# A second copy of each head's high key part: by ScalarE before, by a DMA inside SBUF now

## The chip, the cores and the metric

The kernel runs on one core of one Trainium2 chip, in one launch. The metric is the device time of an execution in microseconds (us). TensorE (PE in the profile, PEld its weight loads), VectorE (DVE), ScalarE (ACT), GpSimd (POOL) and SyncE (SP) run side by side, each through its own list of instructions in order; SP is the engine whose queue starts all of this kernel's DMA transfers.

## The reference, cut to what matters

The kernel computes two decoder layers on 512 tokens of width 1024 in float32: a token mixer, a squared-ReLU MLP and a gated embedding in each layer.

```python
# layer 0: heads A (stick-breaking) and B (differential); layer 1: heads C (three dilated windows)
z  = jnp.einsum('bqhd,bkhd->bhqk', qa_b, ka) * scale          # A
sc = jnp.einsum('bqhmd,bkhmd->bhmqk', qb_b, kb) * scale       # B, plus a bias by distance
sc = jnp.einsum('bqchd,bkchd->bhcqk', q_s, k_s) * scale       # C, plus a bias by distance
...
h = h + mixer(rmsnorm(h)); h = h + square(relu(rmsnorm(h) @ w_up)) @ w_down
h = h + (p @ w_proj) * sigmoid(rmsnorm(h) @ w_gate)
```

Every head has 64 numbers per token for its queries and its keys. The change touches how the keys are laid out for the products q k.

## The kernel before, in words

Every float32 operand is split into a high part, rounded to the format that TensorE multiplies fast (fp32r), and a low part, the rest. Products use three matmuls (high x high, low x high, high x low; `mm3`, L135). ScalarE makes the high part of a weight block (L122) and GpSimd the low part in two halves (L126).

For the scores of a head the parts are stacked instead. A query tile `qq` has 128 partitions: the head's 64 high numbers in one half, its 64 low numbers in the other. The key tile `kh` must then hold the high key part in both halves, so that one matmul gives high x high plus low x high (L498); a second matmul against `klz`, which holds the low key part in one half and zeros in the other, gives the rest (L499). `evacuate` (L462) makes these tiles. Its line L465 takes a product out of PSUM into `f` (`tmp` in the profile): 128 partitions, two heads of 64. For each of the two heads L479 writes the high part into the half where the head lies (`kh[a]`), L480 writes the same numbers into the other half (`kh[b]`), both on ScalarE, and L481 makes the low part on VectorE. Five `kh` buffers take turns.

Each layer's mixer has four groups: layer 0 differential, differential, stick-breaking, stick-breaking; layer 1 four dilated groups. A group projects values, queries and keys (`project`, L401) from three weight blocks of 1 MB and then attends (`attend`, L547): 16 steps of scores, softmax, transposes and products with the values. While one group attends, the projection of the next one runs between its steps (`interleave`, L157). A group has two key products, so four heads, and there are eight groups: L480 runs 32 times. In the first group of a layer the keys come before the values, in all others the keys come last and the group's first scores follow at once.

The framework sets a fixed order for each engine when the kernel is built. TensorE's order mixes the next projection into the scores, and an instruction that must wait holds up all that stands behind it on its engine. On SP the same holds for transfers: a weight load into one of two `raw` buffers (L114) waits until ScalarE and GpSimd have split the block that lay there. Each pair of scores banks in PSUM is freed by VectorE (L515, softmax heads) or ScalarE (L582 and L583, stick-breaking heads). In a differential head `subnorm` (L607) squares on ScalarE (L610, L611) for a matmul over partitions (L614, L615).

Of the kernel before, what the change touches and what calls it, by code (L numbers as in the profile page):

```python
# [12 lines left out]
F32 = mybir.dt.float32  # L13
F32R = mybir.dt.float32r
I32 = mybir.dt.int32
AF = mybir.ActivationFunctionType
# [46 lines left out]
def trunk(  # L63
# [5 lines left out]
    nc = tc.nc  # L69
    uid = [0]  # L70

    def nm(s):
        uid[0] += 1
        return f"{s}_{uid[0]}"
# [15 lines left out]
    def t2k(tag, pool=None, dtype=F32):  # L90
        return (pool or (mix[0] if tag in ("tmp", "tmp2") else spool)).tile([P, S], dtype, tag=tag, name=nm(tag), bufs=T_BUFS.get(tag, 2))
# [274 lines left out]
    def mixer(layer, norm, nxt):  # L366
# [34 lines left out]
        def project(g, cur):  # L401
# [38 lines left out]
            def queries_keys():  # L440
                qscale = -0.5 * HD ** -0.5 if kind == "sb" else 0.5 * HD ** -0.5
                qk, waiting = [], []
                for isq in (True, False):
                    src = next_block()
                    lo_eng[0] = nc.vector if start else nc.gpsimd
                    blk = blk0 if isq and start and not layer else block(src, KT, P)
                    lo_eng[0] = nc.gpsimd
                    accs = [ps_wide() if start else ps("mm") for _ in range(2)]
                    if start and isq:
                        yield from lin_units(accs, blk, ahl, 0, KT, True)  # L450
                        waiting = accs
                        continue
                    for i, acc in enumerate(accs):
                        yield from lin_units([acc], [blk[i]], ahl, 0, KT, False)
                        if waiting:
                            statistics()
                            for x, held in enumerate(waiting):
                                evacuate(True, x, held, qk, qscale)
                            waiting = []
                        evacuate(isq, i, acc, qk, qscale)  # L460

            def evacuate(isq, i, acc, qk, qscale):  # L462
                rstd = stat["rstd"]
                f = t2k("tmp")
                nc.vector.scalar_tensor_tensor(f, acc, qscale if isq else -0.5, rstd, op0=ALU.mult, op1=ALU.mult)  # L465
                lower, upper = slice(0, 64), slice(64, 128)
                if isq:
                    qq = []
                    for a, b in ((lower, upper), (upper, lower)):
                        q = mpool.tile([P, S], F32R, tag="qq", name=nm("qq"), bufs=6)  # L470
                        nc.scalar.activation(q[a], f[a], AF.Copy)
                        nc.vector.tensor_tensor(q[b], f[a], q[a].bitcast(F32), op=ALU.subtract)
                        qq.append(q)
                    qk.append(qq)
                else:
                    for s, (a, b) in enumerate(((lower, upper), (upper, lower))):
                        kl = klz[s][kl_i[0] % KLB]
                        kh = mpool.tile([P, S], F32R, tag="kh", name=nm("kh"), bufs=5)
                        nc.scalar.activation(kh[a], f[a], AF.Copy)  # L479
                        nc.scalar.activation(kh[b], f[a], AF.Copy)  # L480
                        nc.vector.tensor_tensor(kl[a], f[a], kh[a].bitcast(F32), op=ALU.subtract)  # L481
                        heads.append((qk[i][s], kh, kl))
                    kl_i[0] += 1
# [535 lines left out]
```

## Time and profile before

| | us |
|---|---|
| three timed runs | 1310.06, 1311.92, 1312.02 |
| their median | 1311.92 |
| the profiled execution, whole | 1310.61 |
| its span from first to last instruction | 1308.8 |
| TensorE busy in the span | 1285.2 (98%) |
| VectorE busy | 977.6 (75%) |
| ScalarE busy | 687.5 (53%) |
| GpSimd busy | 193.0 (15%) |

The span is cut into 40 slices on the profile's page; TensorE shows 9 tenths or more in all but the last one, so what a change is worth lies in TensorE's short waits. The two mixers lie in about 15 to 255 us and 670 to 890 us of the span. An engine that is busy half of the time can still decide a wait where its instructions bunch: ScalarE shows 6 and 7 tenths in the slices of the first mixer. Bracketed text behind a row of the timeline is the engine's idle time before that instruction and who ended it.

### The profile page before, as it was taken

The page shows a single profiled execution, that of the slowest core. Times are in us where ns is not written, and L with a number is a line of the kernel's source. Part 1 is how long each engine was busy: PE and PEld are TensorE (multiplying, and loading weights), DVE is VectorE, ACT ScalarE, POOL GpSimd, SP SyncE. Part 2 cuts the span into 40 slices and gives each one's busy share as a digit, 9 for nine tenths or more (in the row PEclk, how much of TensorE's full clock was granted, in tenths as well). Part 3 has the DMA queues.
Part 4 walks back from the last instruction along what each step waited for, and adds up shares of the span by engine and source line. Part 5 has one row for each costly group of instructions (what it writes and reads, how often), then busy time and mean ns, then how long its engine had stood idle before and what let it go on. Part 6 is the DMA issues. An engine that isn't in the chain of part 4 may idle for free.

```text
span 1308.8 us, 18582 instructions
## 1 busy us (share of the span) xinstructions
PE 1285.2 (98%) x7256; PEld 1120.1 (86%) x7256; DVE 977.6 (75%) x1623; ACT 687.5 (53%) x1117; POOL 193.0 (15%) x160
## 2 busy tenths in 40 slices
PE   9999999999999999999999999999999999999997
PEld 7888797888998989988889899878899898898886
DVE  6688788768848859845667887887785785994566
ACT  6676768555535334244456667765453443433344
POOL 2333443410000000000023333322000000000001
PEclk9999999999999999999999999999999999999999
DMA  5421323223232322322433222212323223132241
GB/s 204 137 83 57 121 89 113 81 97 118 76 129 68 123 100 97 110 96 87 161 119 105 89 90 74 73 65 70 124 96 104 91 97 127 67 129 97 97 145 65
DMA packets 28040, 133.20 MB, mean 102 GB/s; under 512 B 3312, under 2 KB 4048, under 8 KB 15280
## 3 DMA queue, kind: packets, MB, share of 16 engines
q1 hardware_dynamic: 27952, 132.01, 29.1%
q8 instruction: 57, 0.93, 0.3%
q14 instruction: 31, 0.25, 0.1%
HBM read 125.63 MB, written 6.37 MB: 101 GB/s over the span
## 4 chain that ended last, share of the span: by engine, by line
PE 86%; DVE 7%; ACT 5%; issue 1%; DMA 1%; SPq 0%; DVEq 0%; ACTq 0%
PE mm L136 14%; PE mm L137 14%; PE mm L138 14%; PE tp L138 5%; PE tp L137 5%; PE tp L136 5%; PE sc L138 5%; PE sc L137 5%; PE sc L136 5%; PE pv L543 2%; PE tp L524 2%; PE pv L138 2%; PE pv L137 2%; PE pv L136 2%; PE sc L498 1%; PE sc L499 1%
## 5 line engine op out<-in xcount | busy, mean ns | idle before, releaser
L122 ACT ACTIVATE wh<-raw 128x1024 fp32r<-128x1024 f32 (+1 forms) x168 | 173.6, 1037 | 238.2 <-PE mm L137 74.6
L126 POOL TENSOR_TENSOR wl<-raw,wh 128x512 fp32r<-128x512 f32 (+1 forms) x132 | 180.2, 1388 | 309.2 <-ACT wh L122 290.0
L136 PE MATMUL mm<-hi,wh 128*128 128x512 f32 x564 | 222.8, 395 | 0.0
L137 PE MATMUL mm<-lo,wh 128*128 128x512 f32 x564 | 221.0, 392 | 0.6 <-DVE lo L177 0.6
L138 PE MATMUL mm<-hi,wl 128*128 128x512 f32 x564 | 220.9, 392 | 0.3 <-DVE wl L128 0.3
L128 DVE TENSOR_TENSOR wl<-raw,wh 128x1024 fp32r<-128x1024 f32 x102 | 124.4, 1222 | 40.6 <-ACT wh L122 34.1
L138 PEld LDWEIGHTS mm<-hi,wl 128*128 128x128 f32 x564 | 106.0, 188 | 23.8 <-DVE wl L128 0.7
L137 PEld LDWEIGHTS mm<-lo,wh 128*128 128x128 f32 x564 | 106.2, 188 | 20.9 <-DVE lo L177 1.3
L136 PEld LDWEIGHTS mm<-hi,wh 128*128 128x128 f32 x564 | 106.3, 188 | 20.2 <-ACT hi L176 0.7
L743 ACT ACTIVATE wh<-raw 128x1024 fp32r<-128x1024 f32 x48 | 50.7, 1057 | 69.8 <-PE sc L137 35.4
L138 PE MATMUL mm<-uh,wl 128*128 128x256 f32 (+1 forms) x288 | 87.3, 303 | 0.0
L137 PE MATMUL mm<-ul,wh 128*128 128x256 f32 (+1 forms) x288 | 87.1, 302 | 0.0
L136 PE MATMUL mm<-uh,wh 128*128 128x256 f32 (+1 forms) x288 | 86.4, 300 | 0.0
L518 ACT ACTIVATE e<-e,mn 128x128 f32<-128x128 f32 (+3 forms) x96 | 53.7, 560 | 43.5 <-DVE mn L515 43.2
L722 DVE TENSOR_TENSOR ul<-u,uh 128x1792 fp32r<-128x1792 f32 (+1 forms) x32 | 58.3, 1823 | 23.4 <-ACT uh L721 23.4
L721 ACT ACTIVATE uh<-u 128x1792 fp32r<-128x1792 f32 (+1 forms) x32 | 49.4, 1543 | 48.7 <-DVE u L717 48.4
L710 ACT ACTIVATE u<-u 128x512 f32<-128x512 f32 x64 | 39.4, 624 | 54.3 <-DVE u L709 51.3
L744 DVE TENSOR_TENSOR wl<-raw,wh 128x1024 fp32r<-128x1024 f32 x48 | 58.5, 1220 | 9.8 <-ACT wh L743 9.7
L138 PE MATMUL sc<-hi,wl 128*128 128x512 f32 x168 | 65.4, 389 | 0.0
L137 PE MATMUL sc<-lo,wh 128*128 128x512 f32 x168 | 65.4, 389 | 0.0
L136 PE MATMUL sc<-hi,wh 128*128 128x512 f32 x168 | 65.4, 389 | 0.0
L137 PE MATMUL mm<-wl,hi 128*128 128x256 f32 (+1 forms) x216 | 64.5, 299 | 0.7 <-DVE wl L128 0.7
(261 smaller groups left out, 3467.8 us busy)
## 6 DMA issues: line engine op xcount, KB each, us to landing
raw<-in_w_up_dram SPq DMA_DIRECT2D x32, 1024.0 KB, 4.9
raw<-in_w_down_dram SPq DMA_DIRECT2D x32, 1024.0 KB, 4.9
raw<-in_w_in_dram SPq DMA_DIRECT2D x23, 1024.0 KB, 4.9
raw<-in_w_gate_dram SPq DMA_DIRECT2D x8, 1024.0 KB, 4.9
bias<-urow SPq DMA_DIRECT2D x24, 256.0 KB, 3.5
raw<-in_w_outa_dram SPq DMA_DIRECT2D x8, 768.0 KB, 4.2
pj<-pjd SPq DMA_DIRECT2D x16, 256.0 KB, 4.7
h<-in_xT_dram SPq DMA_DIRECT2D x8, 256.0 KB, 5.6
```

The source lines that it names most:

```text
L122: nc.scalar.activation(hi, src, AF.Copy)
L126: nc.gpsimd.tensor_tensor(lo[:, kx], src[:, kx], hi[:, kx].bitcast(F32), op=ALU.subtract)
L128: nc.vector.tensor_tensor(lo, src, hi.bitcast(F32), op=ALU.subtract)
L136: nc.tensor.matmul(acc, lh, rh, start=start, stop=False)
L137: nc.tensor.matmul(acc, lh, rl, start=False, stop=False)
L138: nc.tensor.matmul(acc, ll, rh, start=False, stop=stop)
L518: nc.scalar.activation(e[:, 0:n], e[:, 0:n], AF.Exp, scale=-1.0, bias=mn, accum_out=s)
L710: nc.scalar.activation(ui, ui, AF.Square, scale=0.5)
L721: nc.scalar.activation(uh[:, parts], u[:, parts], AF.Copy)
L722: nc.vector.tensor_tensor(ul[:, parts], u[:, parts], uh[:, parts].bitcast(F32), op=ALU.subtract)
L743: nc.scalar.activation(hi, src, AF.Copy)
L744: nc.vector.tensor_tensor(lo, src, hi.bitcast(F32), op=ALU.subtract)
```

## The change

L480 becomes a DMA issued by SP. It copies the finished high part from its own half of the tile (`kh[a]`) to the other (`kh[b]`), 64 partitions of 2 KB, 128 KB in all. ScalarE loses 32 instructions, SP's queue gains 32 transfers, and each transfer waits for L479 of its head.

```diff
                         kh = mpool.tile([P, S], F32R, tag="kh", name=nm("kh"), bufs=5)
                         nc.scalar.activation(kh[a], f[a], AF.Copy)
-                        nc.scalar.activation(kh[b], f[a], AF.Copy)
+                        nc.sync.dma_start(kh[b].bitcast(F32), kh[a].bitcast(F32))
                         nc.vector.tensor_tensor(kl[a], f[a], kh[a].bitcast(F32), op=ALU.subtract)
```

The fixed order of the engines shifts with it. On ScalarE, in the first group of layer 0, the keys of the first product (`kh_348`, `kh_352`) and of the second (`kh_382`, `kh_386`) stand around the split of a weight block (`wh_665`):

```order
 L471 ACTIVATE qq_343<-tmp_338 64x512
 L479 ACTIVATE kh_348<-tmp_346 64x512
-L480 ACTIVATE kh_348<-tmp_346 64x512
 L479 ACTIVATE kh_352<-tmp_346 64x512
-L480 ACTIVATE kh_352<-tmp_346 64x512
 L122 ACTIVATE wh_665<-raw_547 128x1024
 L479 ACTIVATE kh_382<-tmp_380 64x512
-L480 ACTIVATE kh_382<-tmp_380 64x512
 L479 ACTIVATE kh_386<-tmp_380 64x512
-L480 ACTIVATE kh_386<-tmp_380 64x512
```

The split and the second product's keys have two copies fewer ahead of them, and what follows has four fewer.

On ScalarE again, where the third group of layer 0 starts, the output of a differential head (`o_206`) and its square (`tmp_328_1604`) stand behind the keys of that group:

```order
 L122 ACTIVATE wh_1641<-raw_1639 128x1024
 L479 ACTIVATE kh_1560<-tmp_1558 64x512
-L480 ACTIVATE kh_1560<-tmp_1558 64x512
 L479 ACTIVATE kh_1564<-tmp_1558 64x512
-L480 ACTIVATE kh_1564<-tmp_1558 64x512
 L597 ACTIVATE o_206<-pv_1571 128x512
 L610 ACTIVATE tmp_328_1604<-o_206 128x512
```

The output and its square have two copies fewer ahead of them.

On SP, where the second group of layer 1 starts (`raw` are weight blocks, `bias` the bias tiles of the scores, `kh_7166` the key tile of the group's first head):

```order
 L507 DMA bias_7498<-urow 128x512
 L114 DMA raw_7672<-in_w_in_dram 128x2048
+L480 DMA kh_7166<-kh_7166 64x512
+L480 DMA kh_7170<-kh_7170 64x512
+L480 DMA kh_7224<-kh_7224 64x512
+L480 DMA kh_7228<-kh_7228 64x512
 L507 DMA bias_7612<-urow 128x512
 L114 DMA raw_7828<-in_w_in_dram 128x2048
```

The four copies stand directly behind a weight load of 1 MB and ahead of the next bias tile. At the start of the third group of layer 1 they stand in the same way behind `raw_8267`, at the start of the fourth behind a load of 768 KB, `raw_8793`.

## Rows read from the trace of the kernel before

**Rows 1.** The page: TensorE's busy time, share of the span, instructions.

```profile
PE 1285.2 (98%) x7256; PEld 1120.1 (86%) x7256; DVE 977.6 (75%) x1623; ACT 687.5 (53%) x1117; POOL 193.0 (15%) x160
```

**Rows 2.** Waits of TensorE: engine, line waited for; us in total, times, longest.

```profile
PE sc L498 <- DVE v L436: 4.0, 2, 2.8
PE sc L498 <- DVE mn L515: 3.9, 4, 1.2
...
PE sc L498 <- ACT e L583: 1.3, 2, 0.9
PE pv L614 <- ACT tmp L611: 1.2, 1, 1.2
...
PE pv L615 <- DVE tmp L612: 0.5, 2, 0.2
```

**Rows 3.** The tile kh: line, engine, count, ns min/median/max, first and last start.

```profile
L480 ACT ACTIVATE kh<-tmp x32: 616/631/634, 39.5 to 851.4; 64x512 fp32r<-64x512 f32 x32
```

**Rows 4.** Windows: stretch, us, busy PE, PEld, DVE, ACT, POOL, PEclk, DMA.

```profile
44.60:48.06 3.46, 0.67 (x6) 0.47 (x5) 2.88 (x5) 2.31 (x5) 0.92 (x1) 1.00 0.39 104
48.06:51.47 3.41, 3.41 (x18) 3.41 (x18) 2.42 (x7) 0.70 (x2) 2.52 (x2) 0.50 0.66 264
704.97:708.40 3.43, 3.43 (x28) 3.43 (x29) 2.33 (x11) 2.00 (x6) 2.56 (x2) 1.00 0.60 248
```

**Rows 5.** Timeline, first group, ScalarE, GpSimd, VectorE, TensorE: start, us, instruction, [idle before].

```profile
41.42 1.06 ACT L122 ACTIVATE wh<-raw 128x1024 fp32r<-128x1024 f32 x1
...
42.56 2.96 POOL L126 TENSOR_TENSOR wl<-raw,wh 128x512 fp32r<-128x512 f32 x2 [5.54 <-ACT wh L122]
...
43.07 2.99 DVE L481 TENSOR_TENSOR klz<-tmp,kh 64x512 fp32r<-64x512 f32 x2 [0.69 <-ACT kh L479]
...
47.66 0.39 PE L498 MATMUL sc<-kh,qq 128*128 128x256 f32 x1 [2.79 <-DVE v L436]
```

**Rows 6.** Timeline, the same group a little later, VectorE and TensorE.

```profile
54.62 0.29 DVE L515 CUSTOM_DVE_ANT_0 e<-sc,bias 128x128 f32<-128x128 f32 x1 [2.46 <-DMA bias<-urow]
...
56.34 0.28 PE L498 MATMUL sc<-kh,qq 128*128 128x256 f32 x1
```

**Rows 7.** Timeline, TensorE's waits at later places of both mixers.

```profile
145.34 0.49 PE L614 MATMUL pv<-tmp,ones_r 128*128 128x512 f32 x1 [1.18 <-ACT tmp L611]
...
704.97 0.36 PE L498 MATMUL sc<-kh,qq 128*128 128x256 f32 x1 [1.20 <-DVE v L436]
...
852.83 0.44 PE L498 MATMUL sc<-kh,qq 128*128 128x384 f32 x1 [1.12 <-DVE mn L515]
```

**Rows 8.** Timeline of SP, the issues of one weight load and one small load.

```profile
45.54 0.35 SPq L114 DMA_DIRECT2D raw<-in_w_in_dram  x1
46.13 0.35 SPq L323 DMA_DIRECT2D tmp<-in_lambdas_dram  x1
```

**Rows 9.** Transfers issued in 45 to 52 us: count, KB each, us to landing.

```profile
raw<-in_w_in_dram SPq DMA_DIRECT2D x1, 1024.0 KB, 5.0
...
tmp<-in_lambdas_dram SPq DMA_DIRECT2D x1, 128.0 KB, 4.7
...
urow<-e SPq DMA_DIRECT2D x2, 8.0 KB, 1.5
```

**Rows 10.** Timeline, starts of layer 1's second and fourth group, SP and TensorE.

```profile
748.34 0.33 SPq L114 DMA_DIRECT2D raw<-in_w_in_dram  x1
...
751.86 0.28 PE L498 MATMUL sc<-kh,qq 128*128 128x256 f32 x1
...
844.12 0.33 SPq L114 DMA_DIRECT2D raw<-in_w_outa_dram  x1
...
848.98 0.28 PE L498 MATMUL sc<-kh,qq 128*128 128x256 f32 x1
```

**Rows 11.** Timeline, start of layer 0's second group, ScalarE and TensorE.

```profile
91.06 0.63 ACT L479 ACTIVATE kh<-tmp 64x512 fp32r<-64x512 f32 x1
...
96.56 0.28 PE L498 MATMUL sc<-kh,qq 128*128 128x256 f32 x1
```

## Prediction

> **What bounds the kernel now.** I read the page's busy times first. TensorE is busy for 98% of the span [rows 1], so an engine that is relieved shortens the kernel only where TensorE waits for it. The second view is therefore the list of TensorE's waits [rows 2]: all of them together are a dozen microseconds, and the groups that could be touched here are the scores (L498) waiting for VectorE's values L436 (4.0 us) and softmax L515 (3.9), the scores waiting for ScalarE's L583 (1.3), and the subnorm matmuls (1.2 and 0.5). The third view, the tile kh, gives the size of what goes [rows 3]. The fourth is the timeline around each of those waits [rows 5 to 7], read backwards: which instruction ended the wait, and do ScalarE's key copies stand ahead of it? Last I read SP's issues and landings [rows 8 to 11], because the copy becomes a transfer there.
>
> **What is removed.** 32 copies of 0.631 us [rows 3] are 20.2 us of ScalarE. Nearly all of it lies beside matmuls and is worth nothing. It counts at these places:
>
> First group of layer 0. TensorE waits 2.79 us for the values L436 [rows 5], which stand on VectorE behind the two low key parts L481. These two take 2.99 us together, and they end about half a microsecond after GpSimd's weight split (42.56 + 2.96 = 45.52 against 43.07 + 2.99 = 46.06), more than twice what ScalarE needs for two of that size; I read this as GpSimd holding VectorE up. GpSimd starts when ScalarE's L122 (41.42, no idle time before it) is done, and two of the removed copies stand right ahead of L122. So the split, the low key parts and the values all move up by 2 x 0.63 = 1.3 us. Gain 1.3, bounds 0 (something else ends VectorE's delay) and 2.6 (all four removed copies count).
>
> Behind that wait TensorE's granted clock is 0.50 for 3.41 us [rows 4], the lower of its two levels (1.2 instead of 2.4 GHz): 1.7 us lost. Ahead of it TensorE had been busy for only 0.67 of 3.46 us. With a wait of 1.5 us I expect the clock to stay up, since behind the wait of 1.20 us that ends at 704.97 [rows 7] it was 1.00 [rows 4]; between 1.2 and 2.8 us nothing shows where it turns. The gain is not all kept. The third pair of scores (56.34) needs a PSUM bank that L515 frees at 54.62 + 0.29 = 54.9, and L515 waited for its bias tile [rows 6]. TensorE would now arrive 3.0 us earlier, at 53.3. The bias comes earlier too: the load at 45.54 that leads its chain of transfers was released by the split ending at 45.52 and moves up by 1.3, but two key copies now stand between, 0.3 each (below), so 0.7 is left and the bank is free at 54.2. 0.9 is given back: the clock is worth 0.8. Bounds 0 and 1.7.
>
> Third group of layer 0. L614 waits 1.18 us for L611 [rows 7], and on ScalarE two removed copies stand shortly ahead of L611, with no idle time between them and it. 1.3 earlier: the wait goes, 1.2. The same chain one group earlier has only the short L615 waits: 0.5 [rows 2].
>
> Stick-breaking starts. Scores wait twice for L583, 1.3 us together [rows 2]; two removed copies stand ahead of L583 on ScalarE each time. All 1.3 goes.
>
> Layer 1. The first group repeats the pattern of layer 0's: 1.20 us for L436 [rows 7], gone with 1.3 earlier: 1.2. At 852.83 the scores wait 1.12 for L515. The split moves up in the same way, but in the new order of VectorE one more low key part (1.5 us, half of the 2.99 in rows 5, if GpSimd hinders it, less if not) stands ahead of L515, so I take 0.4, between -0.4 (1.1 less 1.5) and 1.1.
>
> The rest of the 3.9 us on L515 lies behind VectorE's own work or a bias transfer: 0. Sum of the gains: 1.3 + 0.8 + 1.2 + 0.5 + 1.3 + 1.2 + 0.4 = 6.7 us.
>
> **What is added.** 32 transfers of 128 KB. No row shows one inside SBUF. From below the nearest is a write of 8 KB out of SBUF, 1.5 us to landing; from above a load of the same 128 KB, 4.7 us, but that one was issued behind a 1 MB load [rows 9]. I take 2.2, nearer to the lower end, since the 4.7 is mostly the load ahead. The room: the tightest start without a weight load ahead is layer 0's second group, where L479 of the second head ends at 91.06 + 0.63 = 91.69 and its scores start at 96.56 [rows 11], 4.9 us. ScalarE finishes that head 0.63 earlier than before, TensorE arrives with at most the gains so far. 2.2 fits there, and heads that are used later have 8 us and more. These cost nothing; the cover is the next projection's last matmuls.
>
> Behind a weight load it is different. The 1 MB load issued at 45.54 landed after 5.0 us, at 50.54; the 128 KB load issued at 46.13 landed at 50.83 [rows 8, 9]. So the small one came 0.3 us behind the large one although it is an eighth of its size: transfers of SP's queue finish in turn. In layer 1's second group the four copies stand right behind the load issued at 748.34, which waits for a weight split and is moved by nothing here. It lands at 753.3, the first copy at 753.6, and the scores that need it came at 751.86 [rows 10]. TensorE stands for 1.8 us, and with it the whole next projection queued behind L498. The third group has the same distance, one more: 3.6 together. Nothing later takes it back, since TensorE hardly waits in these groups. In the fourth group the load is issued at 844.12 and the scores come at 848.98 [rows 10]; were that load of 768 KB as slow as 1 MB, the copy would land at 849.4, 0.4 too late; scaled to its size, in time. I take 0.2. Bounds of these three: 0 (the copy overtakes the load) and 5.5 (0.5 more each, for reading and writing SBUF). What stands behind the copies on SP are bias tiles and loads that were issued after the keys were ready anyway, so SP's new waits hold nothing up.
>
> The Trainium skill ("DMA: Bandwidth & Descriptors", section "Anatomy of one DMA") fits a transfer by 2.0 us plus its bytes at 436 GB/s, measured on GpSimd's path; an estimate from it for 128 KB is 2.3 us, and with no regard to the queue the copy would land before the scores come and the sum would be the 6.7 us alone. The load's own 4.7 us [rows 9] is against applying it here, and I go by the rows.
>
> **Sum.** -6.7 + 3.8 = -2.9 us against the profiled execution's 1310.61 (span 1308.8 and 1.8 around it): 1307.7. The median of the runs, 1311.92, lies 1.3 above that execution, so against it 1307.7 is 4.2 less (0.32%); against the execution itself 0.22%.
>
> **Rivals.**
> A. The copies don't queue behind the weight loads, and land 1.5 to 2.5 us after issue: 748.67 + 2.5 = 751.2, in time. Against it the pair of rows 8 and 9. 1310.6 - 6.7 = 1303.9.
> B. ScalarE was not what those waits hung on. VectorE has its own chain at each of them, and the slow low key parts may be slow for another reason. For it: three of the five kinds of waits name VectorE. If half of the gains come, 3.3, and the stalls do, the time is 1311.1: no change.
> C. The new stalls drop the clock. The wait of 2.79 us was followed by 0.50; two waits of 1.8 us might be, at 1.7 us each: 1307.7 + 3.4 = 1311.1, no change. The Trainium skill ("TensorE: Matmul & The Clock Gate", section "What's actually happening") has the lower level as the default that activity lifts, which the stretch in rows 4 agrees with; it makes this likelier than the rows alone.
> D. Slower: a copy inside SBUF is itself slow. The place is the first head of every group that starts with keys last; the point is 4.9 us from issue to landing less the 0.5 to 1.3 that TensorE arrives earlier, about 4.2. At 6 us the three other such starts of layer 0 and layer 1's first lose some 1.5 each, 6 in all, and the three behind loads about 1.2 more each, 3.6: 1307.7 + 9.6 = 1317.3. For it only that no such transfer is in the trace; against it, 1.5 us for the nearest write.
>
> **Chances.** About 0.2% (2.6 us) is what a measurement of this kernel can tell from no change. Forecast 45% (range 1305 to 1310; four fifths of it faster, the rest within 0.2%), A 13% (faster), B 20% (mostly the same, a sixth slower), C 12% (three quarters the same, a quarter slower), D 10% (slower). Faster 0.50, the same 0.34, slower 0.16. The range 1302.5 to 1313.5 holds all but D and the tails of A and C.
>
> **What would show it.** Right: L614 in the third group without its 1.2 us of idle time; L498 of the first group waiting about 1.5 us and no stretch at 0.50 behind it; L583 no longer named among TensorE's waits; and two new waits of TensorE of about 1.8 us in layer 1, on the transfer kh, each with a 1 MB load landing 0.3 us earlier. Wrong: no such transfer waits (A), waits on kh in layer 0 as well (D), L436 and L611 waits unchanged in size (B), or stretches of 0.50 behind the new waits (C).

## The result, and the profile after

The change made the kernel slower: 1314.62 us (median of 12 runs, 1312.69 to 1317.36) against 1311.97 (12 runs of before, 1309.49 to 1314.63), a ratio of 1.0025 with a 95% interval of 1.0016 to 1.0033. Predicted were 1307.7 and a range up to 1313.5. The profiled execution of after took 1314.88 us, its span 1313.1; that of before 1310.61 and 1308.8. The span is 4.2 us longer (4.24 before rounding).

ScalarE was relieved as intended. The first fence is the page of after, engines' busy time, which answers to [rows 1]:

```profile
PE 1288.1 (98%) x7256; PEld 1123.5 (86%) x7256; DVE 976.2 (74%) x1623; ACT 668.7 (51%) x1085; POOL 191.6 (15%) x160
```

ScalarE lost 32 instructions and 18.8 us. TensorE runs the same 7256 matmuls, but is busy 2.9 us longer: some of them ran at the lower clock.

The waits of TensorE in after (us in total, times, longest) answer to [rows 2]:

```profile
PE sc L498 <- DMA kh<-kh: 5.8, 2, 3.0
PE sc L498 <- DVE mn L515: 3.5, 5, 1.2
PE sc L498 <- DVE v L436: 1.6, 1, 1.6
...
PE pv L615 <- DVE tmp L612: 0.2, 1, 0.2
```

Of the waits on which the prediction counted, L583 and L614 are no longer in the list at all, L436 has shrunk from 4.0 us in two waits to 1.6 in one, and a new one heads the list: twice about 3 us for the copied half of kh.

The same line L480 as in [rows 3], now SP's, of after:

```profile
L480 SPq DMA_DIRECT2D kh<-kh x32: 461/467/629, 39.8 to 855.2; - x32
...
DMA to landing us min/median/max: 2.1/3.9/7.1
```

SP spends 0.47 us on issuing one. From issue to landing a copy takes 2.1 us at best and 7.1 at worst.

TensorE at the starts of layer 1's second and third group in the timeline of after. The first of these rows answers to the scores at 751.86 in [rows 10]:

```profile
743.30 0.33 SPq L114 DMA_DIRECT2D raw<-in_w_in_dram  x1
743.73 4.82 SPq L480 DMA_DIRECT2D kh<-kh  x4
...
750.03 0.39 PE L498 MATMUL sc<-kh,qq 128*128 128x256 f32 x1 [3.03 <-DMA kh<-kh]
...
803.07 0.58 PE L498 MATMUL sc<-kh,qq 128*128 128x256 f32 x1 [2.82 <-DMA kh<-kh]
```

And the transfers issued in 743 to 749 us of after (count, KB each, median us to landing):

```profile
raw<-in_w_in_dram SPq DMA_DIRECT2D x1, 1024.0 KB, 6.2
kh<-kh SPq DMA_DIRECT2D x4, 128.0 KB, 5.5
```

The first copy was issued at 743.73 and landed at 749.98, 0.50 behind the load, which landed at 749.48. The load itself took 6.18 us. The load at the same place before took 4.92:

```profile
raw<-in_w_in_dram SPq DMA_DIRECT2D x1, 1024.0 KB, 4.9
```

Windows of after around the new waits (stretch, us, busy PE, PEld, DVE, ACT, POOL, PEclk, DMA share, GB/s), to be read beside [rows 4]:

```profile
747.00:750.00 3.00, 0.00 (x0) 0.00 (x0) 2.81 (x3) 1.03 (x2) 2.30 (x2) 1.00 0.96 285
751.45:754.87 3.42, 3.42 (x19) 3.42 (x18) 1.29 (x6) 0.60 (x2) 0.00 (x0) 0.50 0.00 0
754.87:758.00 3.13, 3.13 (x25) 3.08 (x25) 1.15 (x4) 0.88 (x3) 0.00 (x0) 1.00 0.00 0
...
802.65:806.07 3.42, 3.00 (x14) 3.00 (x15) 0.92 (x4) 0.49 (x2) 0.00 (x0) 0.50 0.17 43
```

TensorE does nothing for 3 us, and behind that the granted clock is 0.50 (1.2 GHz) for 3.4 us, at both places. Before, the only such stretch with matmuls in it was the one of [rows 4] at 48.06; after has one there as well, from 48.30.

**The account.** TensorE runs the same matmuls in both, in the same order but for one place (at 153 us three matmuls of the next projection stand ahead of a pair of scores in after), so the start of one in after less its start in before tells how far after lies behind (+) or ahead (-) there. Each line is worked out from two starts:

| place (time in before) | after less before, us | change |
|---|---|---|
| 10.00, start-up | +0.25 | |
| 94.21, L614 in the first group | -0.36 | -0.61 |
| 94.94, L615 | -0.85 | -0.49 |
| 145.34, L614 | -2.10 | -1.25 |
| 287.97, end of layer 0's mixer | -3.79 | -1.69 |
| 704.97, first group of layer 1 | -5.02 | -1.23 |
| 751.86, first wait for kh | -1.83 | +3.19 |
| 755.56, behind the half clock | -0.23 | +1.60 |
| 800.34, second wait for kh | +2.73 | +2.96 |
| 802.00, behind the half clock | +4.16 | +1.43 |
| 848.98, fourth group | +4.42 | +0.26 |
| 856.24, behind L515's wait | +3.64 | -0.78 |
| end of the execution | +4.27 | +0.63 |

Down to 704.97 the change is worth 5.0 us. Two places take 9.2 us. The account is of the two profiled executions, which are 4.27 us apart; the medians are 2.65 apart, since the profiled execution of before lies 1.36 below its median and that of after 0.26 above.

### The profile page after: what moved, and what is told of

Same layout as the page of the kernel before. It is cut to its first block, busy times and chain, and to the rows that moved or that the text cites. A ratio compares the mean times of both kernels' runs of the same rounds, so it can differ in the third digit from the quotient of the medians.

```text
span 1313.1 us, 18641 instructions
## 1 busy us (share of the span) xinstructions
PE 1288.1 (98%) x7256; PEld 1123.5 (86%) x7256; DVE 976.2 (74%) x1623; ACT 668.7 (51%) x1085; POOL 191.6 (15%) x160
## 4 chain that ended last, share of the span: by engine, by line
PE 87%; DVE 5%; ACT 3%; DMA 2%; issue 1%; SPq 0%; POOL 0%; ACTq 0%; DVEq 0%
PE mm L136 14%; PE mm L137 14%; PE mm L138 14%; PE tp L138 5%; PE tp L137 5%; PE tp L136 5%; PE sc L138 5%; PE sc L137 5%; PE sc L136 5%; PE pv L543 3%; PE pv L137 2%; PE pv L138 2%; PE tp L524 2%; PE pv L136 2%; PE sc L498 2%; PE sc L499 1%
## 5 line engine op out<-in xcount | busy, mean ns | idle before, releaser
L136 PE MATMUL mm<-wh,hi 128*128 128x256 f32 (+1 forms) x216 | 65.7, 305 | 0.0
```

Source lines behind the costliest of these rows:

```text
L136: nc.tensor.matmul(acc, lh, rh, start=start, stop=False)
```

## The experiments

All times are medians, the ratios against runs of before on the same chip in the same series (1311.35 in the first series, 1311.2 in the second). The line numbers in a kernel's rows are its own: L501 and L506 are the scores L498, L486 is the copy L480, L523 the softmax L515, L623 the subnorm matmul L615.

**One layer at a time.** If the two layers work as the account says, the change in layer 0 alone is a gain and in layer 1 alone a loss. In layer 0 alone:

```diff
-                        nc.sync.dma_start(kh[b].bitcast(F32), kh[a].bitcast(F32))
+                        if not layer:
+                            nc.sync.dma_start(kh[b].bitcast(F32), kh[a].bitcast(F32))
+                        else:
+                            nc.scalar.activation(kh[b], f[a], AF.Copy)
```

> The copy is a transfer in layer 0 alone; layer 1 keeps ScalarE's copy. Theory: the loss lies where the copies stand behind a weight load and the group's first scores follow at once, which happens in layer 1 alone; layer 0 keeps the 3.8 us that the trace after shows won by its end. So 1308.2 us against 1312.0 before, no wait on kh. Rival: the 16 transfers that are left cost by loading SP's queue as a whole, wherever they stand; then half of the loss stays, 1313.3 us.

Measured: 1306.80 us (6 runs), ratio 0.9969 (0.9957 to 0.9980). That is 4.55 less than before in this series, where the theory had 3.8 and the rival a loss; no wait on kh is in its list.

In layer 1 alone (`if layer:` in the same place):

> The copy is a transfer in layer 1 alone. Theory: 1.25 us won at its first group, 3.1 us of waiting on kh plus 1.4 us at half clock lost at each of the next two groups, about 0.3 at the last: 1319.5 us against 1312.0 before, with two waits on kh of 3 us. Rival (the queue as a whole is slower): 1313.3 us.

Measured: 1318.85 us (5 runs), ratio 1.0058 (1.0045 to 1.0070). The waits of TensorE in this kernel:

```profile
PE sc L501 <- DMA kh<-kh: 6.6, 3, 3.1
```

The window that holds the end of the second of them, and what follows:

```profile
806.08:812.90 6.82, 5.75 (x27) 5.75 (x28) 2.54 (x9) 1.10 (x4) 0.38 (x1) 0.50 0.17 39
```

So the change is worth -4.55 us in layer 0 and costs 7.50 in layer 1, by the medians. The sum, +2.95, agrees with the +2.65 of the whole change within the intervals, about 1.5 us to either side for each kernel. The layers don't add up quite simply: in layer 1 alone the stretch at 0.50 behind the second wait lasts 6.82 us instead of 3.42, which by TensorE's starts costs 2.63 us instead of 1.43. By the prediction's terms the layers were worth -5.1 and +2.2: it is layer 1 that failed.

**The copies ahead of the load.** As after, but at each group of layer 1 the load that stood ahead of the first product's two copies on SP is put behind them; nothing else in the program is changed.

```diff
-        nc.sync.dma_start(raw, src)
+        ld = nc.sync.dma_start(raw, src)
+        for c in ahead:
+            c[1] += 1
+            if c[1] == 3:
+                order(ld.ins, c[0])
...
-                        nc.sync.dma_start(kh[b].bitcast(F32), kh[a].bitcast(F32))
+                        cp = nc.sync.dma_start(kh[b].bitcast(F32), kh[a].bitcast(F32))
+                        if layer and i == 0:
+                            ahead.append([cp.ins, 0])
```

> All copies are transfers, but in layer 1 the weight load behind which the first two copies of a group stood is ordered behind them on SP. Nothing else changes. Theory: no wait on kh at the starts of layer 1's groups and no stretch at half clock behind them, so both losses go and all that was won stays: 1306.5 us against 1312.0 before, 1314.6 for the change. Rival (32 transfers inside SBUF slow the loads in any order): still about 1314 us, the loads still late.

Measured: 1306.12 us (5 runs, 1305.45 to 1306.93), ratio 0.9963 (0.9951 to 0.9976). SP's timeline at the second group, and TensorE's scores there:

```profile
741.02 1.12 SPq L486 DMA_DIRECT2D kh<-kh  x2
743.02 0.34 SPq L114 DMA_DIRECT2D raw<-in_w_in_dram  x1
746.55 0.28 PE L506 MATMUL sc<-kh,qq 128*128 128x256 f32 x1
```

Transfers issued from 740.5 to 744 us in this kernel:

```profile
raw<-in_w_in_dram SPq DMA_DIRECT2D x1, 1024.0 KB, 5.3
kh<-kh SPq DMA_DIRECT2D x2, 128.0 KB, 2.2
```

The copies go out as soon as ScalarE has written their sources, and each takes 2.2 us. The load isn't held up, since GpSimd's split lets it go only at 743.0, as in after; TensorE has no idle time at 746.55 (no bracket), the granted clock stays at 1.00, and the 8.5 us between 1314.62 and 1306.12 are back (8.1 by the two ratios to before, since the two were timed in different series). With the order of two transfers on one queue alone the loss became a gain; the copy itself was never the trouble.

**The copies on another queue.** All copies are issued by ScalarE, `nc.scalar.dma_start` in place of `nc.sync.dma_start`; the loads stay on SP.

> All copies are transfers issued by ScalarE on its own queue instead of SP's. Theory (in SP's queue transfers finish in turn): on another queue the copy need not wait for the load's end, so the wait on kh in layer 1 falls from 3 us to under 1; but ScalarE now spends an issue on each copy (SP needs 0.47 us for one), which takes back most of what its 0.63 us copies had cost: 1310 us against 1312.0 before. Rival (the load and the copies share the engines that move bytes, whatever the queue): the wait on kh stays at 2 to 3 us, 1314 us or more.

Measured: 1306.62 us (5 runs), ratio 0.9965 (0.9951 to 0.9978). This is better than the theory's 1310, which took each issue as 0.47 us of ScalarE against the 0.63 that go. The issues do take that long, but only one of a pair holds ScalarE up. The first is issued while ScalarE writes the second head's half (L479); at the second, ScalarE stands idle for 0.5 to 0.6 us in 13 of the 16 pairs, as here in the first group:

```profile
43.34 0.47 ACTq L480 DMA_DIRECT2D kh<-kh  x1
43.86 0.47 ACT L435 ACTIVATE v<-sc,rcol 128x256 fp32r<-128x256 f32 x1 [0.55 <-ACT kh L479]
```

A pair of copies thus costs ScalarE about 0.55 us, where it had cost 1.26 and the theory left 0.94. How much of the 3.4 us between 1310 and 1306.62 this explains isn't shown. L480 of this kernel:

```profile
L480 ACTq DMA_DIRECT2D kh<-kh x32: 468/468/507, 39.7 to 848.2; - x32
...
DMA to landing us min/median/max: 2.2/2.2/3.2
```

At the second group the copies go out at 742.38, right behind the instructions that make their sources, and the first has landed at 744.62; SP's load is issued at 744.38. So this run, too, brings the copy ahead of the load. Whether a copy on ScalarE's queue overtakes a load that is already under way it doesn't show: the two that were issued into a load, 3.5 us behind its issue, landed 0.8 and 1.8 us after it.

Both runs point to the same second half of the trouble in after. The first copy's source was ready by about 741.3 (ScalarE, after):

```profile
740.64 1.28 ACT L479 ACTIVATE kh<-tmp 64x512 fp32r<-64x512 f32 x2
```

The copy was issued at 743.73, 2.4 us later, since SP issues in order and stood at the load that waited for GpSimd until 743.30.

**What stretches the load.** The load ahead of the copies took 6.2 us instead of 4.9. Three kernels built on before (ScalarE still makes both halves; kh has 4 buffers instead of 5, which was not run by itself) put two transfers of 128 KB right behind the same loads, and nobody waits for these. They differ in where the two come from and go to: from SBUF to SBUF, from SBUF to DRAM, and from DRAM to SBUF.

```diff
...
+                        if layer and i == 0:
+                            if s == 0:
+                                idle[0] = mpool.tile([P, S], F32, tag="idle", name=nm("idle"), bufs=1)
+                            nc.sync.dma_start(idle[0][b], kh[a].bitcast(F32))
```

> The kernel before (ScalarE still makes both halves), with kh in 4 buffers instead of 5, plus two transfers per layer-1 group on SP's queue right behind the weight load that the first product's copies of after stand behind: the upper or lower half of kh, 64 x 512 from SBUF to SBUF, into a spare tile that nobody reads. Theory (transfers of the second halves slow the load that is under way, and cost time only through the wait of the scores): the 1024 KB load near 748 us lands after about 6.1 us instead of 4.92, the one near 797 after about 6.0 instead of 4.93, each copy within 0.6 us behind it, no wait of TensorE on a kh, and the time is that of before, 1311.9 within 2 us. Rival one (the load of after was long for another cause, for instance because it was issued 5 us earlier): the load still takes 4.9 to 5.0. Rival two (the transfers in themselves take SBUF or engine time): 4 us or more above before, though nothing waits for them.

The second kernel has `nc.sync.dma_start(spare[2 * kl_i[0] + s], kh[a].bitcast(F32))` there, `spare` in DRAM:

> As the idle SBUF copies, but the two transfers go from the kh tile to DRAM (64 x 512 each, nobody reads them). If the reading of SBUF behind the load is what stretches it: the load near 748 us takes 6.0 or more. If only a transfer with SBUF at both ends does: 4.9 to 5.5. Time as before, 1311.9 within 3 us, in both.

The third has `nc.sync.dma_start(idle[part], xT[z, part])`, behind ScalarE's last key copy:

> As the idle SBUF copies, but the two transfers of 64 x 512 come from DRAM (a piece of xT) into the spare tile. If any 256 KB queued behind the load stretches it: the load near 748 us takes 6.0 or more. If the source in SBUF is what does it: 4.9 to 5.1, as with the two bias loads behind a weight load in the kernel before. Time as before, 1311.9 within 3 us, in both.

The transfers issued from 748 to 750.5 us, in the order of the three kernels:

```profile
raw<-in_w_in_dram SPq DMA_DIRECT2D x1, 1024.0 KB, 6.1
idle<-kh SPq DMA_DIRECT2D x2, 128.0 KB, 6.8
```

```profile
raw<-in_w_in_dram SPq DMA_DIRECT2D x1, 1024.0 KB, 5.6
spare<-kh SPq DMA_DIRECT2D x2, 128.0 KB, 6.3
```

```profile
raw<-in_w_in_dram SPq DMA_DIRECT2D x1, 1024.0 KB, 5.4
idle<-in_xT_dram SPq DMA_DIRECT2D x2, 128.0 KB, 5.4
```

| behind the load | load near 748, us | load near 797, us | time |
|---|---|---|---|
| nothing for some 10 us (before) | 4.92 | 4.93 | |
| two copies, SBUF to SBUF | 6.13 | 6.05 | 1311.48 (10 runs), ratio 1.0000 (0.9990 to 1.0009) |
| two writes, SBUF to DRAM | 5.58 | 5.37 | 1311.07 (1 run) |
| two reads, DRAM to SBUF | 5.35 | 5.64 | 1311.61 (1 run) |

Two things follow. Copies behind a load lengthen that load by 1.1 to 1.2 us, with ScalarE's work untouched and at the time where before has it, so the first rival of that experiment (the earlier issue) falls. And the eight transfers in themselves cost the kernel nothing beyond the interval of about 1.2 us to either side: only a wait on them does. That the source in SBUF is what does it failed: reads from DRAM lengthen the load as well, to 5.35 and 5.64, where 4.9 to 5.1 was expected. The writes to DRAM, at 5.58 and 5.37, fell short of the 6.0 of one expectation and lie about the upper end of the other's 4.9 to 5.5. Both kinds add 0.4 to 0.7. Why a transfer with both ends in SBUF does more is open.

**The best version.** The copies ahead of the load in layer 1, and the four copies of the very first group on ScalarE's queue:

```diff
-                        cp = nc.sync.dma_start(kh[b].bitcast(F32), kh[a].bitcast(F32))
+                        cp = (nc.scalar if start and not layer else nc.sync).dma_start(kh[b].bitcast(F32), kh[a].bitcast(F32))
```

> As the version with the copies ahead of the load in layer 1, and the four copies of the very first group are issued from ScalarE's queue instead of SP's, so that they don't stand behind the first group's load. Theory (the first group's gain was lost because the load and the transfers for the bias finish behind each other): the load near 45 us takes 4.9 instead of 6.0, the bias lands near 54.0 instead of 56.0, and 0.4 to 0.8 us are gained: 1305.5 where the version it is built on gave 1306.1. Rival (the stretch at half clock after the first wait decides, not the bias): 1306.1 within 0.3 us.

Measured: 1304.24 us (5 runs, 1303.93 to 1305.88), ratio 0.9948 (0.9935 to 0.9960). It is faster than before and than after. Its interval overlaps that of the version it is built on, so the times don't separate the two. In the traces TensorE is 5.99 us ahead of before at 704.97 here and 5.29 there. Transfers issued from 44 to 52 us in it:

```profile
raw<-in_w_in_dram SPq DMA_DIRECT2D x1, 1024.0 KB, 4.9
...
urow<-e SPq DMA_DIRECT2D x2, 32.0 KB, 2.1
```

VectorE's softmax, which waits for the first bias, in this kernel and then in after:

```profile
54.06 0.29 DVE L523 CUSTOM_DVE_ANT_0 e<-sc,bias 128x128 f32<-128x128 f32 x1 [2.47 <-DMA bias<-urow]
```

```profile
55.94 0.29 DVE L515 CUSTOM_DVE_ANT_0 e<-sc,bias 128x128 f32<-128x128 f32 x1 [2.52 <-DMA bias<-urow]
```

With the load back at 4.9 us, the writes behind it that the bias waits for take 2.1 us instead of 4.3, and the softmax comes 1.9 us earlier. The granted clock behind the first group's wait (2.2 us here) is 0.50 all the same, so the prediction's gain from the clock doesn't hang on the bias.

The 0.7 us that this kernel is ahead at 704.97 are the number that was expected, but by luck: they don't come from the first group. It is 0.4 us ahead of the version it is built on at 61 us, 0.2 of it from the start-up, and loses this again at the second group's softmax, which waits for its own bias transfer in both kernels. TensorE's scores behind it, first with the copies ahead of the load alone, then in this kernel:

```profile
114.33 0.38 PE L506 MATMUL sc<-kh,qq 128*128 128x256 f32 x1 [0.86 <-DVE mn L523]
```

```profile
114.36 0.38 PE L506 MATMUL sc<-kh,qq 128*128 128x256 f32 x1 [1.32 <-DVE mn L523]
```

The 0.7 arise behind that, where the third group starts: L623 comes at 143.70 behind a wait of 0.23 us in the one and at 143.08 without a wait in the other. Why the work ahead of it comes sooner there isn't shown, and no run shows that the first group's queue is worth anything in the time of the whole kernel.

## Why the prediction was wrong, point by point

**The waits that go: right.** L614's wait fell as forecast (1.25 us in the account, 1.2 predicted), so did L615's (0.49, 0.5) and that of layer 1's first group (1.23, 1.2). The stick-breaking starts gave 1.69 between 145.34 and 287.97, where 1.3 was predicted. The softmax wait at 852.83 gave 0.78 by 856.24, for which 0.4 was taken. Rival B, that ScalarE was not what these waits hung on, is out; layer 0 alone, at -4.55 us, says the same.

**The copy by itself: right.** "I take 2.2": a copy with nothing ahead of it takes 2.2 us, by the median of the two versions that keep it clear of the loads. So rival D is out, and no scores in layer 0 wait on kh. The Trainium skill's fit ("DMA: Bandwidth & Descriptors", section "Anatomy of one DMA"), of which 2.3 us was an estimate, agrees with this measurement, and says nothing of a copy behind a load.

**The first group: partly wrong.** Predicted were 1.3 from the wait and 0.8 from the clock, 2.1 together; 0.61 was kept. The wait itself shrank by 1.15, from 2.79 to 1.64 us, but "with a wait of 1.5 us I expect the clock to stay up" failed. TensorE's scores behind the wait in after, which answer to the last of [rows 5]:

```profile
46.75 0.38 PE L498 MATMUL sc<-kh,qq 128*128 128x256 f32 x1 [1.64 <-DVE v L436]
```

The first group in windows of after, which answer to the first two of [rows 4]:

```profile
44.80:48.30 3.50, 1.64 (x12) 1.23 (x10) 2.93 (x7) 2.15 (x4) 0.73 (x1) 1.00 0.74 180
48.30:51.72 3.42, 3.35 (x16) 3.38 (x17) 0.76 (x3) 0.00 (x0) 1.77 (x2) 0.50 0.87 261
```

TensorE was busy for 1.64 us of the stretch ahead, instead of 0.67, and the lower level came nevertheless. The other half of the term, the bias, went the wrong way. Its chain of transfers was to come 0.7 us earlier; the load that leads it did start 0.91 earlier (44.63), but with two copies right behind it it took 6.08 us instead of 4.99, and the bias tile landed at 55.79 instead of 54.47. The load in after:

```profile
raw<-in_w_in_dram SPq DMA_DIRECT2D x1, 1024.0 KB, 6.1
```

**The two starts behind a load: the step that failed.** "It lands at 753.3, the first copy at 753.6 ... TensorE stands for 1.8 us ... 3.6 together." The mechanism was there, at the places named, and "transfers of SP's queue finish in turn" held: the copy landed 0.50 us behind the load, where 0.3 was taken. The size was off, 3.19 and 2.96 us instead of 1.8 each, for the sum took the load's own landing as fixed at the 4.9 us it had with nothing behind it. With copies behind, it took 6.18 and 5.97. That is 1.3 and 1.0 us, and 0.2 more for the copy: 1.8 + 1.3 + 0.2 = 3.3 and 1.8 + 1.0 + 0.2 = 3.0, close to the account. The bounds had the same gap: "0.5 more each, for reading and writing SBUF" was added to the copies alone. The probes with idle transfers show the longer load by itself. That the load "is moved by nothing here" was wrong too, without effect: it came 5.04 us earlier, together with TensorE.

**The clock behind them, rival C: the other step that failed.** The sum put nothing for the clock behind these waits, with only the wait of 1.20 us at 704.97 to go by; C had 1.7 us for each. The stretch at 0.50 came behind both and cost 1.60 and 1.43. C was right in kind, and its 1311.1 was too low because it had the waits 2.55 us too short and 1.49 us too much from the first group.

**The third start.** 0.2 was taken at the fourth group; the scores came within 0.05 us of the copy (landed 853.36, scores 853.40). In layer 1 alone, where TensorE came without the gains of layer 0, the third wait was 0.49.

**The sum again.** Predicted were -6.7 + 3.8 = -2.9 us, the account has +4.27. Of the difference of 7.2, 2.55 is the size of the two waits (6.15 against 3.6), 3.03 the clock behind them, 1.49 the first group, 0.06 the third start and 0.88 what the account shows at the start-up and the end, where the change has no step; the stick-breaking starts, L515 and some hundredths elsewhere take 0.84 off. 1307.7 + 7.2 = 1314.9, the profiled execution's 1314.88. The pair of transfers in [rows 9] showed the small one held by the large one; that the large one pays for the small one behind it was the question that wasn't asked.

## What to carry to other kernels

A copy that goes from an engine to a DMA is paid for by its place on the queue, not by its own 2 us: see which load stands ahead of it when its source is ready, and put the copy ahead of that load, or let an engine issue it that doesn't stand at the load. Count the landing of both, since a load with copies right behind it lands later as well (4.9 us became 6.0 and more here). An idle stretch of TensorE of 3 us cost 4.4 to 4.8 here, for the stretch at half clock behind it belongs to the price.

## What the runs showed of the hardware that was not expected

- A 1 MB load took 4.9 us with nothing right behind it on SP's queue and 6.0 to 6.3 with two to four 128 KB copies from SBUF to SBUF behind it (6.3 in layer 1 alone); with writes to DRAM behind it 5.4 to 5.6, with reads from DRAM 5.4 to 5.6.
- The level of 0.50 came behind a wait of 1.64 us (after, 46.75) and did not behind one of 1.20 (before, 704.97). It also came where TensorE's idle time was in pieces: in the version with copies on ScalarE's queue it was busy for 1.87 of 3.41 us, and the clock fell behind that.

```profile
100.10:103.51 3.41, 1.87 (x13) 1.35 (x12) 3.35 (x11) 0.79 (x3) 0.00 (x0) 1.00 0.00 0
103.52:106.93 3.41, 3.41 (x16) 3.41 (x17) 2.22 (x9) 2.45 (x6) 0.20 (x1) 0.50 0.00 0
```
